# The delta heads' base inverses stay on the chip: turned by VectorE and copied into level tiles

## The chip, the cores and the metric

The kernel runs on one core of a Trainium2 chip. The metric is the device time of one launch in microseconds, the median of several runs. The core's engines are TensorE (PE in the profile, its weight loads PEld), VectorE (DVE), ScalarE (ACT), GpSimd (POOL) and SyncE (SP), which issues the transfers of this kernel; 16 DMA engines carry them.

## The reference

One layer of a bidirectional encoder for 1024 tokens of width 1024, in float32: a mixer of windowed attention and gated DeltaNet side by side, then cross-attention into 256 memory tokens, then a SwiGLU block. The change lies in the DeltaNet part, which solves a unit lower triangular system for each head, direction and chunk of 64 tokens:

```python
kb = k * beta[..., None]
lower = jnp.where(strict, jnp.einsum('bhnid,bhnjd->bhnij', kb, k) * decay, 0.0)
tmat = lower + jnp.eye(c, dtype=jnp.float32)
rhs = jnp.concatenate([v * beta[..., None], kb * jnp.exp(g)[..., None]], axis=-1)
sol = lax.linalg.triangular_solve(tmat, rhs, left_side=True, lower=True, unit_diagonal=True)
```

There are 4 heads and 2 directions. The kernel works on blocks of 128 tokens (8 of them, NT), and inverts the triangle instead of solving.

## The kernel before

**Stages.** The first stage projects the delta heads' keys, queries and values, convolves them, and forms the products of keys (`ORDER_1`, up to about 215 us). The second (`ORDER_2`, up to about 370 us) projects the attention heads' columns (`A`), values (`V`) and the delta heads' gates (`G`), runs the first attention windows (`W`) and the levels of the inverses (`L0` to `L3`, one for each head). The third (`ORDER_3`) runs the recurrent scans over the eight blocks, with the remaining windows and the projections of the memory between their steps. Cross-attention and the SwiGLU block follow. The tokens in `ORDER_1` to `ORDER_3` give the order of the program text. A scheduler lays out each engine's instructions ahead of the launch (`schedule_with_timeline_sim=True`); on the chip each engine and SP's queue runs its own instructions in that order.

**Base inverses.** The heads are taken in two groups g of two. `base_inverse(g)` (tokens `B0`, `B1`) inverts all diagonal blocks of 32x32 of a group at once: 2 directions x 2 heads x 8 blocks of 128 tokens x 4 blocks of 32 give 128 systems, one on each partition, in a tile A of [128, 32, 32]. A forward substitution on VectorE (L581 and L583, 30 steps) runs on A in place. Then the unit diagonal is set (L584), and the columns are multiplied by beta twice: on VectorE into V with rows and columns swapped (L585), and on GpSimd into A itself (L586).

**The way through DRAM.** On each partition a block of 32x32 lies along the free dimension. The levels need it with its rows on partitions. For that A and V are written to DRAM tensors: `d_m5` holds blocks of 32x32, and `d_lv` holds images of whole level tiles in which the blocks lie on the diagonal (`diagonal`, L591 to L595; ten issues for each group, in pieces of 32 elements for `d_lv`). All the rest of an image has to be zero, so eight transfers from a zeroed tile clear `d_lv` early in the first stage (`clear`, L453, tokens `Z` in `ORDER_1`). `levels(h)` reads `d_m5` once (L605) and a tile DZ of [128, 4, 4, 128] for each half of the blocks (L615, 1 MB each). DZ holds four images: D5 and D6, the left factors of the two levels, and Z for each direction, which becomes the result.

**Levels.** A part b of `levels(h)` covers four blocks of 128 tokens. It loads the key products Ul (L618), transposes them on TensorE (L622) and masks them into L5 and L6 on VectorE (L623, L624). `pair` is a product with L on TensorE (L631), an eviction on ScalarE (L633), and a product with D5 or D6 (L637). The first pair joins blocks of 32 to 64: z5 (L642) is put into D6 by two VectorE transposes (L643, L644) and into Z by copies (L645, L646, L650, L651). mov6 (L648, L649) is read from Z for the second pair, which joins 64 to 128 and writes the last quarters of Z (L653, L654). Z is stored to `d_pz` (L656) for the scans. The two parts run interleaved, and products of the projections (L289) stand between their steps on TensorE.

**Neighbours.** The rotary embedding of the attention columns (L785 to L792) makes two products on VectorE, swaps halves by four transfers `rr<-rr` (L790), adds (L791) and stores (L792). The gate's activation (L811, L812) uses the same tile tag as the rotary sum. Each projection loads its weights (L125), and splits them in two parts on ScalarE (L103) and VectorE (L104). A window loads its queries (L671), splits them on ScalarE and GpSimd (L673, L674) and goes on with scores on TensorE and VectorE.

## Time and profile before

| | |
|---|---|
| median of three runs | 1529.46 us (1528.9 to 1532.73) |
| the profiled execution | 1530.58 us, span 1528.9 us |
| mean granted TensorE clock | 0.989 |
| DMA | 276.26 MB, mean 181 GB/s |
| packets under 512 B | 39264 of 287335 |
| the first stage's stretch from 20 to 200 us | TensorE busy 179.2 of 180 us |

The profile gives busy time for each engine, and for stretches of time; the times of single instructions on each queue; in brackets the time an engine stood idle ahead of an instruction, and the event that ended this. A matmul's end is modelled, so a TensorE that counts as busy can still lose time: its starts and its clock tell more. "SPq" rows are issues on SP's queue, and their time is what the issue held the queue for.

### The profile page before, as it was taken

To read this page: it belongs to the slowest core of one execution; us is meant where nothing else is said; L and a number is where in the kernel's file an instruction comes from. 1 tells how busy PE (TensorE), PEld (TensorE's weight loads), DVE (VectorE), ACT (ScalarE), POOL (GpSimd) and SP (SyncE) were. 2 spreads that over 40 slices of the span, in tenths; PEclk is the share of its full clock that TensorE was granted. 3 is DMA by queue.
4 is the path that set the end of the run, shared out by engine and by line. 5 is a ranking of instruction groups with operands and counts; after the bars stand their busy time and mean duration, and the time that the engine had idled before them with its cause. 6 is when DMAs were issued, how large, how long until landed. Compare 5 with 4: busy or idle time off the path is not lost.

```text
span 1528.9 us, 21239 instructions
## 1 busy us (share of the span) xinstructions
PE 1479.8 (97%) x7437; PEld 1244.3 (81%) x7437; DVE 1092.5 (71%) x1795; ACT 756.5 (49%) x1556; POOL 329.9 (22%) x301
## 2 busy tenths in 40 slices
PE   7999999899999999999999999999999999999998
PEld 6888877787999778888788867888888888888787
DVE  5878998466888866538567768676867775696666
ACT  7678821346567755455545685223232332454533
POOL 0011210101237203152201101433434342000020
PEclk9999999899999999999999999999999999999999
DMA  6844596975998675458734654343434333853355
GB/s 192 298 117 128 146 242 187 235 206 177 336 308 260 199 240 184 134 170 274 237 102 162 203 178 132 104 138 111 149 105 160 124 103 105 321 208 98 109 177 167
DMA packets 287335, 276.26 MB, mean 181 GB/s; under 512 B 39264, under 2 KB 211453, under 8 KB 287229
## 3 DMA queue, kind: packets, MB, share of 16 engines
q1 hardware_dynamic: 287229, 274.92, 57.0%
q8 instruction: 58, 0.95, 0.3%
q14 instruction: 48, 0.39, 0.1%
HBM read 187.54 MB, written 84.71 MB: 178 GB/s over the span
## 4 chain that ended last, share of the span: by engine, by line
PE 64%; DVE 7%; DMA 7%; SPq 3%; issue 2%; ACT 2%; POOL 1%; DVEq 0%; ACTq 0%; POOLq 0%
PE pE L1509 7%; PE pD L1509 7%; PE pmg L1099 6%; PE pdX L1715 6%; PE pA L1509 6%; PE pst L1315 5%; PE pcq L289 4%; PE pdA L1715 4%; PE pB L1509 3%; PE psc L838 3%; PE pdD L1715 2%; PE pg L289 2%; PE pco L1214 1%; DMA qr<-d_q 1%; DMA wraw<-in_w_gate_up_dram 1%
## 5 line engine op out<-in xcount | busy, mean ns | idle before, releaser
L103 ACT CAST whi<-wraw 128x1024 fp32r<-128x1024 f32 x96 | 100.8, 1050 | 133.4 <-DMA wraw<-in_w_gate_up_dram 39.8
L289 PE MATMUL pg<-hhi,whi 128*128 128x512 f32 x352 | 142.2, 404 | 0.0
L289 PE MATMUL pg<-hlo,whi 128*128 128x512 f32 x352 | 142.2, 404 | 0.0
L289 PE MATMUL pg<-hhi,wlo 128*128 128x512 f32 x352 | 140.7, 400 | 0.0
L104 POOL TENSOR_TENSOR wlo<-wraw,whi 128x1024 fp32r<-128x1024 f32 x36 | 88.4, 2455 | 190.1 <-ACT whi L103 181.5
L1509 PE MATMUL pA<-b,whi 128*128 128x512 f32 x352 | 110.9, 397 | 3.6 <-ACT m L1536 2.8
L104 DVE TENSOR_TENSOR wlo<-wraw,whi 128x1024 fp32r<-128x1024 f32 x60 | 73.6, 1227 | 45.2 <-ACT whi L103 44.1
L1509 PEld LDWEIGHTS pA<-b,whi 128*128 128x128 f32 x352 | 65.8, 189 | 18.9 <-ACT m L1536 4.1
L289 PEld LDWEIGHTS pg<-hhi,whi 128*128 128x128 f32 x352 | 67.9, 193 | 13.5 <-ACT hhi L254 0.3
L289 PEld LDWEIGHTS pg<-hhi,wlo 128*128 128x128 f32 x352 | 67.8, 193 | 12.9
L289 PEld LDWEIGHTS pg<-hlo,whi 128*128 128x128 f32 x352 | 67.6, 192 | 12.5
L1715 PE MATMUL pdX<-dhl,whi 128*128 128x512 f32 x264 | 76.1, 390 | 1.5 <-DVE zv L1774 0.7
L1509 PE MATMUL pA<-b,wlo 128*128 128x512 f32 x176 | 69.4, 395 | 0.5 <-DVE wlo L104 0.5
L103 ACT CAST whi<-araw 128x1024 fp32r<-128x1024 f32 (+1 forms) x36 | 35.3, 981 | 67.7 <-PE pdX L1715 27.6
L1592 POOL TENSOR_TENSOR act<-act,up 128x512 f32<-128x512 f32 x33 | 50.7, 1537 | 82.1 <-DVE up L1591 60.8
L104 DVE TENSOR_TENSOR wlo<-araw,whi 128x1024 fp32r<-128x1024 f32 (+1 forms) x36 | 40.8, 1133 | 36.7 <-ACT whi L103 36.5
L314 DVE SCALAR_TENSOR_TENSOR acc<-cp,cols,acc 128x1024 f32<-128x1024 f32 x48 | 63.7, 1330 | 1.5 <-ACT acc L312 1.2
L1564 POOL TENSOR_TENSOR sr<-wraw 128x512 f32<-128x512 f32 x22 | 29.9, 1360 | 151.8 <-DMA wraw<-in_w_gate_up_dram 100.3
L1715 PEld LDWEIGHTS pdX<-dhl,whi 128*128 128x128 f32 x264 | 49.3, 188 | 12.7 <-issue 1.1
L103 ACT CAST dhl<-b 128x512 fp32r<-128x512 f32 x66 | 40.3, 620 | 31.7 <-PE pdA L1715 13.5
L1509 PE MATMUL pB<-s0h,s1h 128*128 128x512 f32 x176 | 54.4, 390 | 0.3 <-ACT s1h L103 0.3
L1509 PE MATMUL pE<-b,s2h 128*128 128x512 f32 x176 | 54.2, 389 | 0.0
(495 smaller groups left out, 4199.7 us busy)
## 6 DMA issues: line engine op xcount, KB each, us to landing
wraw<-in_w_gate_up_dram SPq DMA_DIRECT2D x54, 512.0 KB, 3.8
kv<-d_kv SPq DMA_DIRECT2D x32, 512.0 KB, 8.0
wraw<-in_w_in_dram SPq DMA_DIRECT2D x22, 512.0 KB, 6.5
b<-in_w_down_dram SPq DMA_DIRECT2D x20, 512.0 KB, 6.0
araw<-d_as SPq DMA_DIRECT2D x20, 512.0 KB, 3.6
d_lv<-zero SPq DMA_DIRECT2D x8, 1024.0 KB, 8.9
DZ<-d_lv SPq DMA_DIRECT2D x8, 1024.0 KB, 8.9
pz<-d_pz SPq DMA_DIRECT2D x32, 256.0 KB, 6.5
```

Of the source, the lines that this page charges most:

```text
L103: nc.scalar.copy(hi, src)
L104: return (eng or nc.vector).tensor_tensor(lo, src, f32(hi), ALU.subtract)
L289: nc.tensor.matmul(p_, w[:, k, :], ah[a][:, k, :], start=(k == 0 and i == 0), stop=(k == nk - 1 and i == 2))
L314: nc.vector.scalar_tensor_tensor(acc, cp[:, t:t + S], taps[t], acc, ALU.mult, ALU.add)
L838: nc.tensor.matmul(out[:, d, h, :], lt[:, d, h, :], rt[:, d, h, :], start=True, stop=True)
L1099: nc.tensor.matmul(pp[t], act[a][:, k, tt], w_[:, kk, :], start=(k == 0 and i == 0), stop=(k == KT - 1 and i == 2))
L1214: nc.tensor.matmul(po, vr_[a][:, kt, cs], pts[kt][b_], start=(kt == 0 and i == 0), stop=(kt == 1 and i == 2))
L1315: nc.tensor.matmul(bank, a[:, tt], w, start=(start and i == 0), stop=(stop and i == 2), skip_group_check=not check)
L1509: nc.tensor.matmul(out_, w[a][:, k, :], xx[b_][:, k, :], start=(start and k == 0 and i == 0), stop=(k == HK - 1 and i == 2), skip_group_ch ...
L1564: nc.gpsimd.tensor_tensor(s[0], b_[:, 0:HK], b_[:, HK:], ALU.add)
L1592: nc.gpsimd.tensor_tensor(o_, o_, up, ALU.mult)
L1715: nc.tensor.matmul(banks[t], a[:, k - k0, tt], w, start=(first and k == 0 and i == 0), stop=(k == NB - 1 and i == 2), skip_group_check=not ...
```

## The change

In `base_inverse` the multiplication by beta is done once, on VectorE and in place in A, and the unit diagonal is set there too. `turn_base` makes two tiles of it, `turned_base[0]` and `[1]`, with one VectorE transpose of 32x32 blocks each, one of them reading A with rows and columns swapped. For group 0 it is called at the end of `base_inverse(0)`, for group 1 at the head of `levels(2)`. `block_of` gives the view of these tiles that holds one block for several chunks; its elements are 32 apart.

The DRAM tensors `d_lv` and `d_m5` go, with the clears, the scatter and the loads. m5 is filled by four ScalarE copies for each level. The images D, Z0 and Z1 of each half are tiles that exist once for the whole stage and are cleared once on GpSimd. D serves both levels: four ScalarE copies set its diagonal blocks for the first pair, and between the pairs two GpSimd copies replace its second and third block. From the second head on, the two corners that the level before has filled are cleared again. Eight GpSimd copies set the diagonals of Z0 and Z1.

The rest is room: a pool `wt` holds A and the two turned tiles, shared with `abT` and with the work tiles of the rotary angles, the positions are loaded in one transfer, V has one buffer for both groups, and z5 and mov6 have two buffers each.

```diff
@@ -34,7 +34,7 @@
 
 
 
-ORDER_1 = ("k0 k1 Z E0 Z K0 Z U0 Z E1 Z K1 Z U1 Z S0 q0 Z v0 q1 C0 v1 E2 C1 k2 E3 k3 q2 K2 U2 v2 K3 U3 S1 q3 C2 v3 C3 B0 B1").split()
+ORDER_1 = ("k0 k1 E0 K0 U0 E1 K1 U1 S0 q0 v0 q1 C0 v1 E2 C1 k2 E3 k3 q2 K2 U2 v2 K3 U3 S1 q3 C2 v3 C3 B0 B1").split()
 ORDER_2 = "L0 L1 A4 V A0 A1 G0 G1 L2 L3 W W W A2 A3 G2 G3 W".split()
 ORDER_3 = ("M " + "s01 W K " * 5 + "s01 K " * 3 + "s01 V V").split()
 
@@ -148,6 +148,7 @@
     p1 = ExitStack()
     hx = p1.enter_context(pool("hx", 1, side="right"))
     trp = p1.enter_context(pool("trp", 2, side="right"))
+    wt = p1.enter_context(pool("wt", 1, side="right"))
     pcv = ExitStack()
     tcv = pcv.enter_context(pool("tcv", 2, side="right"))
     pa0 = ExitStack()
@@ -185,20 +186,6 @@
     d_pz = [[dram.tile([NT, P, 2, 2, P], F32, name=f"d_pz{g}{d}") for d in range(2)] for g in range(2)]
     d_u = [dram.tile([2, NT, P, P], F32, name=f"d_u{g}") for g in range(2)]
 
-    LW, LB_ = 4 * P, 32 * 4 * P + 32
-    d_lv = [dram.tile([1, 8 * NT * LB_ + LW], F32, name=f"d_lv{g}") for g in range(2)]
-    d_m5 = [dram.tile([8 * NT, 32, 32], F32, name=f"d_m5{g}") for g in range(2)]
-
-    def diagonal(g, kind):
-
-        at = kind * P
-        return (d_lv[g][0, at:at + 8 * NT * LB_].rearrange("(n y) -> n y", y=LB_)[:, 0:32 * LW]
-                .rearrange("n (r w) -> n r w", w=LW)[:, :, 0:32])
-
-    def level_rows(g, x0):
-
-        return (d_lv[g][0, 0:8 * NT * LB_].rearrange("(x y) -> x y", y=4 * LB_)[x0:x0 + 4, 0:P * LW]
-                .rearrange("x (p w) -> p x w", w=LW))
     d_beta = [dram.tile([32, P], F32, name=f"d_beta{g}") for g in range(2)]
     d_mix = dram.tile([D, S], F32, name="d_mix")
     d_mk = dram.tile([D, ML], F32, name="d_mk")
@@ -339,7 +326,7 @@
         nc.vector.tensor_scalar(wabr, hT[0][0].bitcast(F32)[:, :, 0:P], 0.0, None, ALU.mult)
     nc.vector.tensor_copy(wabr[:, :, 0:16], wab)
     nc.vector.tensor_tensor(wabr[:, :, 16:32], wab, f32(wabr[:, :, 0:16]), ALU.subtract)
-    abT = tb.tile([32, S], F32, tag="A", name="abT", bufs=1)
+    abT = wt.tile([32, S], F32, tag="A", name="abT")
     for hf in range(2):
         pp = pg.tile([P, 512], F32, tag="pg", name="pg")
         for k in range(KT):
@@ -409,14 +396,14 @@
     c3 = float(np.float32(2 * math.pi - c1 - c2))
     sct = ra.tile([P, 2, S], F32, tag="sct", name="sct")
     sinT, cosT = sct[:, 0], sct[:, 1]
+    posi = wt.tile([P, S], I32, tag="inv1", name="posi")
+    nc.sync.dma_start(posi, positions[0].partition_broadcast(P))
     for hf in range(2):
         sl = slice(hf * HALF, (hf + 1) * HALF)
-        posi = t1.tile([P, HALF], I32, tag="posi", name="posi", bufs=1)
-        nc.sync.dma_start(posi, positions[0, sl].partition_broadcast(P))
-        ang = t1.tile([P, HALF], F32, tag="ang", name="ang", bufs=1)
-        nc.vector.tensor_copy(ang, posi)
+        work = wt.tile([P, 2, HALF], F32, tag="inv0", name="ang")
+        ang, rn = work[:, 0], work[:, 1]
+        nc.vector.tensor_copy(ang, posi[:, sl])
         nc.vector.tensor_scalar(ang, ang, rope_f, None, ALU.mult)
-        rn = t1.tile([P, HALF], F32, tag="rn", name="rn", bufs=1)
         nc.vector.tensor_scalar(rn, ang, 1.0 / (2.0 * math.pi), MAGIC, ALU.mult, ALU.add)
         nc.vector.tensor_scalar(rn, rn, MAGIC, None, ALU.subtract)
         for cc in (c1, c2, c3):
@@ -430,7 +417,6 @@
 
     pa1.close()
     pa0.close()
-    tb1 = pp_.enter_context(pool("tb1", 1))
 
 
 
@@ -442,15 +428,6 @@
     nEG = sm.tile([P, 2, 4, NT], F32, name="nEG")
     nc.vector.tensor_scalar(nEG, EG[:, 0], -1.0, None, ALU.mult)
 
-    zero = t2.tile([P, 4, P], F32, tag="vt", name="zero").rearrange("p c n -> p (c n)")
-    nc.gpsimd.memset(zero, 0.0)
-    cleared = [0]
-
-    def clear():
-
-        g, x0 = cleared[0] // 4, 4 * (cleared[0] % 4)
-        cleared[0] += 1
-        nc.sync.dma_start(level_rows(g, x0), bc(zero, 1, (P, 4, LW)))
 
 
     def together(gens):
@@ -558,7 +535,7 @@
 
 
 
-        V = (tb1 if g else tb).tile([P, 32, 32], F32, tag="V", name="V", bufs=1)
+        V = tb.tile([P, 32, 32], F32, tag="V", name="V", bufs=1)
         for q in range(4):
             r = slice(32 * q, 32 * q + 32)
             nc.sync.dma_start(V[q:64:4], d_u[g].rearrange("h c p n -> (h c) p n")[:, r, r])
@@ -568,7 +545,7 @@
         for d in range(2):
             nc.sync.dma_start(bB[64 * d:64 * d + 64], bv[d])
         nc.sync.dma_start(b1, bv[1])
-        A = tb.tile([P, 32, 32], F32, tag="A", name="A", bufs=1)
+        A = wt.tile([P, 32, 32], F32, tag="A", name="A")
         nc.vector.scalar_tensor_tensor(A[0:64], V[0:64].rearrange("p r s -> p s r"), -1.0,
                                        bc(bB[0:64], 1, (64, 32, 32)), ALU.mult, ALU.mult)
         nc.vector.scalar_tensor_tensor(A[64:128], V[0:64], -1.0, bc(b1, 1, (64, 32, 32)), ALU.mult, ALU.mult)
@@ -581,18 +558,25 @@
             nc.vector.tensor_tensor(tv, A[:, j + 1:, j:j + 1].to_broadcast([P, n, j]),
                                     A[:, j:j + 1, 0:j].to_broadcast([P, n, j]), ALU.mult)
             nc.vector.tensor_tensor(A[:, j + 1:, 0:j], A[:, j + 1:, 0:j], tv, ALU.add)
-        nc.gpsimd.memset(A.rearrange("p r s -> p (r s)")[:, 0:1024:33], 1.0)
-        nc.vector.tensor_tensor(V.rearrange("p r s -> p s r"), A, bc(bB, 2, (P, 32, 32)), ALU.mult)
-        nc.gpsimd.tensor_tensor(A, A, bc(bB, 2, (P, 32, 32)), ALU.mult)
-
-        for d in range(2):
-            first, second = (A, V) if d == 0 else (V, A)
-            lo_, hi_ = 64 * d, 64 * d + 64
-            nc.sync.dma_start(d_m5[g][1 - d::2], second[lo_ + 1 - d:hi_:2])
-            nc.sync.dma_start(diagonal(g, 0)[d::2], first[lo_ + d:hi_:2])
-            nc.sync.dma_start(diagonal(g, 2 + d), second[lo_:hi_])
-            for q in (2 * d, 2 * d + 1):
-                nc.sync.dma_start(diagonal(g, 1)[q::4], first[lo_ + q:hi_:4])
+        nc.vector.memset(A.rearrange("p r s -> p (r s)")[:, 0:1024:33], 1.0)
+        nc.vector.tensor_tensor(A, A, bc(bB, 2, (P, 32, 32)), ALU.mult)
+        bases.append(A)
+        if g == 0:
+            turn_base()
+
+    bases, turned_base = [], []
+
+    def turn_base():
+
+        turned_base[:] = [wt.tile([P, 32, 32], F32, tag=f"inv{i}", name=f"inv{i}") for i in range(2)]
+        A = bases.pop()
+        nc.vector.transpose(turned_base[1], A)
+        nc.vector.transpose(turned_base[0], A.rearrange("p r s -> p s r"))
+
+    def block_of(kind, d, hh, b, cs):
+
+        q = 64 * d + 32 * hh
+        return turned_base[kind][q:q + 32].rearrange("p x (c b) -> p b c x", b=4)[:, b, cs]
 
     def levels(h):
 
@@ -601,8 +585,11 @@
         def blocks(name):
             return tl_.tile([P, NT, 32], F32, tag=name, name=name, bufs=1)
 
+        if bases and h == 2:
+            turn_base()
         m5 = blocks("m5")
-        nc.sync.dma_start(m5, d_m5[g][32 * hh:32 * hh + 32].rearrange("(c b) r s -> (b r) c s", b=4))
+        for q in range(4):
+            nc.scalar.copy(m5[32 * q:32 * q + 32], block_of(q % 2, 1 - q % 2, hh, q, slice(0, NT)))
 
         def part(b):
             c4 = slice(4 * b, 4 * b + 4)
@@ -611,9 +598,21 @@
                 return tl_.tile([P, 4, P], F32, tag=name, name=name, bufs=2)
 
             L5, L6 = wide("L5"), wide("L6")
-            DZ = tl_.tile([P, 4, 4, P], F32, tag="DZ", name="DZ", bufs=3)
-            nc.sync.dma_start(DZ.rearrange("p c k n -> p c (k n)"), level_rows(g, hh * NT + 4 * b))
-            D5, D6, Z = DZ[:, :, 0], DZ[:, :, 1], [DZ[:, :, 2 + d] for d in range(2)]
+            D5, *Z = images[b]
+            D6 = D5
+
+            def put(copy, dst, q, kind, d):
+                x = slice(32 * q, 32 * q + 32)
+                copy(dst[x, :, x], block_of(kind, d, hh, q, c4))
+
+            if h:
+                nc.gpsimd.memset(D5[32:64, :, 0:32], 0.0)
+                nc.gpsimd.memset(D5[64:96, :, 96:128], 0.0)
+            for q in range(4):
+                put(nc.scalar.copy, D5, q, q % 2, q % 2)
+            for d in range(2):
+                for q in range(4):
+                    put(nc.gpsimd.tensor_copy, Z[d], q, 1 - d, d)
             Ul = wide("Ul")
             nc.sync.dma_start(Ul, d_u[g][hh, c4].rearrange("c p n -> p c n"))
             yield
@@ -638,13 +637,15 @@
                 return p_
 
             p_ = yield from pair(L5, m5[:, c4, :], D5, 32)
-            z5 = tl_.tile([P, 4, 32], F32, tag="z5", name="z5", bufs=1)
+            z5 = tl_.tile([P, 4, 32], F32, tag="z5", name="z5", bufs=2)
             nc.scalar.mul(z5, p_, -1.0)
+            put(nc.gpsimd.tensor_copy, D6, 1, 0, 0)
+            put(nc.gpsimd.tensor_copy, D6, 2, 1, 1)
             nc.vector.transpose(D6[32:64, :, 0:32], z5[0:32])
             nc.vector.transpose(D6[64:96, :, 96:128], z5[96:128])
             nc.vector.tensor_copy(Z[1][32:64, :, 0:32], z5[32:64])
             nc.vector.tensor_copy(Z[0][64:96, :, 96:128], z5[64:96])
-            mov6 = tl_.tile([P, 4, 64], F32, tag="mov6", name="mov6", bufs=1)
+            mov6 = tl_.tile([P, 4, 64], F32, tag="mov6", name="mov6", bufs=2)
             nc.scalar.copy(mov6[0:64], Z[1][0:64, :, 0:64])
             nc.vector.tensor_copy(mov6[64:128], Z[0][64:128, :, 64:128])
             nc.scalar.copy(Z[0][0:32, :, 32:64], z5[0:32])
@@ -758,9 +759,8 @@
         for o in order:
             table[o[0]](*(int(c) for c in o[1:]))
 
-    issue(ORDER_1, {**{n: delta_proj(n) for n in "kqv"}, "Z": clear, "E": decays, "K": turned_keys, "U": key_products, "S": beta_rows,
+    issue(ORDER_1, {**{n: delta_proj(n) for n in "kqv"}, "E": decays, "K": turned_keys, "U": key_products, "S": beta_rows,
                     "C": query_products, "B": base_inverse})
-    assert cleared[0] == 8
     pp_.close()
     pcv.close()
     pss.close()
@@ -770,6 +770,9 @@
     tw.tile([P, 384], F32, tag="sc", name="sc", bufs=8)
     vhl = tw.tile([P, NT + 1, 2, 2, 64], F32R, tag="vhl", name="vhl", bufs=1)[:, 0:NT]
     tl_ = p1.enter_context(pool("tl", 2))
+    images = [[tl_.tile([P, 4, P], F32, tag=f"{n}{b}", name=n, bufs=1) for n in ("D", "Z0", "Z1")] for b in range(2)]
+    for t in images[0] + images[1]:
+        nc.gpsimd.memset(t, 0.0)
 
     def pair():
         t = ra.tile([P, 2, HALF], F32, tag="rr", name="rr", bufs=2)
```

## The prediction

> **What bounds the kernel now.** I read the busy table and the slices first, then the stretches of 20 us around the edit, then each TensorE stop there with the queue behind it.
>
> ```profile
> PE 1479.8 (97%) x7437; PEld 1244.3 (81%) x7437; DVE 1092.5 (71%) x1795; ACT 756.5 (49%) x1556; POOL 329.9 (22%) x301
> ```
>
> TensorE is the bound, and the edit leaves its matmuls as they are in number and shape. So it can only give or take TensorE's stops and the low clock behind them. The stretches (columns: length, busy of PE, PEld, DVE, ACT, POOL with counts, granted clock, DMA share, GB/s):
>
> ```profile
> 40.00:60.00 20.00, 20.00 (x93) 16.10 (x92) 19.55 (x30) 10.51 (x16) 0.27 (x4) 1.00 1.03 373
> 60.00:80.00 20.00, 20.00 (x96) 16.75 (x95) 14.36 (x28) 14.73 (x29) 0.13 (x2) 1.00 0.57 181
> 200.00:220.00 20.00, 20.00 (x95) 16.28 (x94) 19.55 (x28) 5.79 (x21) 3.89 (x4) 1.00 0.87 192
> 220.00:240.00 20.00, 17.03 (x87) 14.35 (x87) 15.26 (x35) 2.24 (x7) 0.00 (x0) 0.91 1.05 312
> 240.00:260.00 20.00, 19.45 (x108) 16.22 (x106) 17.89 (x45) 4.54 (x11) 0.15 (x1) 1.00 0.37 104
> 260.00:280.00 20.00, 18.61 (x101) 15.34 (x99) 12.33 (x19) 4.74 (x9) 1.92 (x1) 1.00 0.95 226
> 280.00:300.00 20.00, 15.91 (x78) 13.46 (x78) 6.24 (x18) 9.35 (x24) 2.74 (x3) 0.82 0.94 263
> 300.00:320.00 20.00, 20.00 (x107) 17.39 (x107) 11.92 (x29) 7.68 (x23) 2.79 (x3) 0.93 0.82 235
> ```
>
> From 200 to 320 us, where the levels run, TensorE stands idle 2.97 + 0.55 + 1.39 + 4.09 = 9.0 us. The clock of 0.91, 0.82 and 0.93 costs at most 0.09, 0.18 and 0.07 of 20 us each, 6.8 us; part of that falls on idle time, so I count 6. DMA is near its full share in the same stretches. The four long stops, in brackets with their releasers, and what stood in front of them on SP, ACT, DVE and POOL:
>
> ```profile
> 223.05 0.66 PE L622 MATMUL ps<-ident,Ul 128*128 128x128 f32 x4 [2.97 <-DMA Ul<-d_u]
> 265.73 0.66 PE L622 MATMUL ps<-ident,Ul 128*128 128x128 f32 x4 [1.39 <-DVE DZ L654]
> 281.20 1.10 PE L631 MATMUL ps<-mov,L 128*128 128x64 f32 x8 [1.15 <-ACT mov L648]
> 297.18 1.12 PE L622 MATMUL ps<-ident,Ul 128*128 128x128 f32 x4 [2.48 <-DVE DZ L654]
> ```
>
> ```profile
> 197.60 0.49 SPq L591 DMA_DIRECT2D d_m<-V  x1
> 205.80 1.34 SPq L595 DMA_DIRECT2D d_lv<-V  x1
> 217.22 0.45 SPq L618 DMA_DIRECT2D Ul<-d_u  x1
> 264.52 4.27 SPq L592 DMA_DIRECT2D d_lv<-V  x1
> 272.44 2.81 SPq L595 DMA_DIRECT2D d_lv<-V  x2
> 276.52 0.53 SPq L792 DMA_DIRECT2D d_q<-rop  x1
> 281.38 0.58 SPq L615 DMA_DIRECT2D DZ<-d_lv  x1
> ```
>
> ```profile
> 279.64 0.60 ACT L811 ACTIVATE gt<-pg 128x512 f32<-128x512 f32 x1 [5.52 <-DMA d_q<-rop]
> 295.77 0.62 ACT L673 CAST qs<-qr 128x512 fp32r<-128x512 f32 x1 [2.23 <-DMA qr<-d_q]
> ```
>
> ```profile
> 262.75 1.92 POOL L586 TENSOR_TENSOR A<-A,bB 128x1024 f32<-128x1024 f32 x1 [3.40 <-DMA d_pz<-DZ]
> 254.92 0.69 DVE L791 TENSOR_TENSOR rop<-rop,rr 128x512 f32<-128x512 f32 x1 [0.27 <-DMA rr<-rr]
> 263.17 2.04 DVE L791 TENSOR_TENSOR rop<-rop,rr 128x512 f32<-128x512 f32 x1 [0.51 <-DMA rr<-rr]
> ```
>
> The reader is to see that all four lead back to work which the edit removes. **Stop one**: Ul is issued only at 217, after SP has spent 197.6 to 207.1 on the scatter of base 0, and lands beside the first DZ loads. **Stop two**: the rope add takes 2.04 us where it else takes 0.69, since it stands until POOL's multiply L586 ends at 262.75 + 1.92 = 264.67; L654 and the release of the PSUM bank follow it. **Stop three**: the gate's activation waits for the store d_q, held on SP to 276.5 behind the scatter of base 1, and mov of the level is behind it on ACT. **Stop four**: ACT waits for a window's qr load with DMA full (0.94), a DZ load of 1 MB among it, and the level's last step is behind that wait.
>
> **The change part by part.**
>
> *Clears.* Eight issues of 1 MB each go from the front.
>
> ```profile
> d_lv<-zero SPq DMA_DIRECT2D x8, 1024.0 KB, 8.9
> DZ<-d_lv SPq DMA_DIRECT2D x8, 1024.0 KB, 8.9
> ```
>
> At 40 to 60 us they fill DMA (1.03), but TensorE is busy for all 20.00 us, so I take 0. PEld is 16.10 against 16.75 in the next stretch, 0.65 us that could be hidden loss: bounds 0 and -0.8. Positions in one load and the shared tiles change no count of DVE work there: 0.
>
> *Scatter and DZ loads.* Twenty scatter issues, four m5 and eight DZ loads go. Their worth is the stops: -9.0 - 6 = **-15 us** if nothing takes their place. The bound below it is the 0.8 of the clears on top.
>
> *DVE.* A base loses the multiply L585 and gains the contiguous multiply, a small memset and two transposes.
>
> ```profile
> L585 DVE TENSOR_TENSOR V<-A,bB x2: 2070/2082/2093, 195.5 to 260.6; 128x1024 f32<-128x1024 f32 x2
> L104 DVE TENSOR_TENSOR wlo<-wraw,whi x8: 1194/1221/1626, 197.4 to 318.0; 128x1024 fp32r<-128x1024 f32 x8
> L643 DVE STREAM_TRANSPOSE DZ<-z x8: 301/301/302, 242.5 to 351.9; 32x128 f32<-32x128 f32 x8
> L645 DVE COPY DZ<-z x8: 216/217/219, 243.5 to 352.6; 32x128 f32<-32x128 f32 x8
> ```
>
> The contiguous multiply is like wlo, 1.22. No transpose of 1024 columns is shown: at the least it is one pass like wlo, 1.22; at the most eight of the small ones, 8 x 0.301 = 2.41. The one that reads with a stride I put by L585, 2.08, the other at 1.3, since the small one is 0.08 above the copy of its size. With 0.1 for the memset that is 1.22 + 0.1 + 1.3 + 2.08 - 2.08 = **+2.6 us** a base, bounds +1.7 and +4.1. DVE is busy 19.55 of 20 around base 0, so rope work behind it comes 2.6 later; TensorE did not wait for it there (20.00), so 0 to +2.6, and I take 0. In exchange POOL's 2.32 us multiply leaves the chain, and with it stop two.
>
> *ACT.* Sixteen copies of 32x256 for m5 and 32 of 32x128 for D.
>
> ```profile
> L648 ACT COPY mov<-DZ x8: 390/406/407, 243.8 to 357.5; 64x256 f32<-64x256 f32 x8
> L650 ACT COPY DZ<-z x8: 280/298/300, 238.8 to 351.9; 32x128 f32<-32x128 f32 x8
> ```
>
> 16 x 0.41 + 32 x 0.30 = 16 us. Their read has a stride that these rows lack; twice that, 32 us, is the other bound (DVE's L585 is 1.7 times its contiguous kin). ACT is busy 2.2 to 9.4 of 20 us here, which covers either sum. Without the cover each level pays 4 us ahead of its first pair. The copies into D wait for the last matmul that reads it in the level before, as its only image now; behind a wait of that kind stand weight casts and evictions on ACT.
>
> *POOL.* Sixty-four copies into Z, sixteen into D between the two pairs, 12 memsets of corners, six whole ones.
>
> ```profile
> L674 POOL TENSOR_TENSOR qs<-qr,qs 64x512 fp32r<-64x512 f32 x8 | 10.4, 1297 | 81.3 <-ACT qs L673 80.9 <-DVE nm L689 0.4
> 298.19 0.20 POOL L694 TENSOR_TENSOR es<-prm,m 128x4 f32<-128x4 f32 x1 [0.47 <-DVE m L684]
> L446 POOL MEMSET zero<- 128x512 f32 x1 | 0.5, 524 | 0.0
> 259.19 0.15 POOL L584 MEMSET A<- 128x32 f32 x1 [44.06 <-DVE A L583]
> ```
>
> A tiny operation is 0.20, and 128 columns of L674's 512 are 0.32: bounds 0.20 and 0.52, and I take 0.4 for one copy. 80 x 0.4 + 12 x 0.15 + 6 x 0.52 = 37 us over some 150, on an engine that stood idle for 44 us there. Eight copies, 3.2 us, stand ahead of a part's mov, beside its transpose and first pair. If they are late, TensorE stops at L631, since its order is fixed. The copies into Z also wait for the store d_pz of the level before; nothing but windows' qs (1.30 each) stands behind them. Base 1's transposes wait on DVE until L1's copies have read the turned tiles, with rope adds and the masks L623 behind them, which TensorE needs for its next bank.
>
> Here is the weak spot: POOL and DVE. Stop two showed a DVE add waiting for POOL's whole instruction. So 80 copies can hold up DVE, and be held up by it. In place of the four stops I put two new ones, one for each pair of levels, of the mean size of the old, 15 / 4 = 3.75 us: **+7.5 us**. Bounds: none, and the rival below.
>
> The Trainium skill has a rule on this, in "SBUF — State Buffer", section "Who interferes with whom": a VectorE instruction with two SBUF inputs and a GpSimd instruction that reads SBUF exclude each other for the whole instruction, and the second to start stands still. The trace agrees (2.04 us for 0.69). It speaks against copies on POOL beside the long DVE loop of base 1; by it the sum would be that of the lock's rival below, 1536 us, and by the rows' mean stop 1522.
>
> *The sum* is made against the profiled execution: 1530.6 us, with a span of 1528.9, against a median of 1529.5; the differences of 1.1 and less do not matter. -15 + 7.5 = -7.5, so 1529.5 - 7.5 = **1522 us**.
>
> **The rivals.** *Full gain.* The levels run from engines alone, POOL keeps up, no new stop: 1529.5 - 15 = 1514.5 us. For it:
>
> ```profile
> L637 PE MATMUL ps<-bs,DZ x128: 190/275/323, 237.4 to 366.3; 128*128 128x32 f32 x64, 128*128 128x64 f32 x64
> L583 DVE TENSOR_TENSOR A<-A,tmpb x60: 191/346/410, 136.5 to 260.3; 128x30 f32<-128x30 f32 x4, 128x58 f32<-128x58 f32 x4, 128x84 f32<-128x84 f32 x4, 128x108 f32<-128x108 f32 x4
> ```
>
> Base 0 is ready for its multiplies at 195.5 (L585's first start), but its first product with D runs at 237.4, 42 us later, most of it spent on the way through DRAM. DMA loses 8 MB of loads there, and by the code 2 x 8,192 pieces of 128 bytes. Against: the order on TensorE is fixed ahead, so any late copy is a stop.
>
> *Stops handed on.* The transfers were hidden in effect: with them gone, TensorE stops at the next late thing (Ul, qr and the rope's rr loads are still there, DVE is at 19.55) and the 15 us come back: 1529.5 us, 1525 to 1534. That SP and DMA stand in three of the four stops speaks against it.
>
> *The lock, on the other side.* DVE's loop of base 1, up to 260.3, is one of small two-input adds, and each POOL copy waits for one and holds up the next. With a wait of 0.4 (an add of L583 takes 0.35 to 0.41) a part's eight copies take 6.4 us in place of 3.2. That decides where mov comes later than its slot on TensorE. At 3.2 us a part, half covered, eight parts give 13 us idle, and the low clock (6 us for 9 before) adds 8: 13 + 8 - 15 = +6, so 1536 us; with no cover 26 + 17 - 15 = +28. For it: stop two. Against: base 1's loop ends before L2, so half of the parts see less of it.
>
> **How the numbers follow.** Full gain 0.20, forecast 0.33 (1517 to 1525), handed on 0.15, lock 0.32. What a measurement here can tell from no change is 0.3%, 4.6 us, so the line of faster is 1524.9 and of slower 1534.1. Faster: 0.20 + 0.32 of the forecast; same: 0.15 and the forecast's last 0.01; slower 0.32. The range takes in full gain with a bit of the clears and a copy or two less late, 1511, and the lock to less than half of its uncovered price, 1542; less than 0.2 is outside. The likeliest case's own range is 1517 to 1525.
>
> **What would show it.** Right: no stop before L622 on Ul at the first level; SP without 1 to 4 us issues at 197 to 207 and 264 to 275; DMA share of 200 to 320 near 0.5; clock 1.00 but for one or two dips. Copies of 0.4 on POOL, transposes of 1.3 and 2.1 on DVE. The lock: DVE adds of L583 well over 0.4 beside POOL copies, copies over 0.6, and stops at L631 released by mov. The prediction is wrong if TensorE's idle time from 200 to 320 does not fall below 9 us, or if the time is lost after 380 us, where the scans run.

## The result and the profile after

The changed kernel takes 1537.74 us (median of four runs, 1535.31 to 1540.26) where the kernel before takes 1529.18 us (four runs). The ratio is 1.0053, with a 95% interval of 1.0028 to 1.0078: slower by 0.53%, 8 us, where the forecast was 1522. The profiled execution is one of 1540.26 us with a span of 1538.0 us and a mean granted clock of 0.989, the same clock as before.

The page of the kernel after, busy time of each engine:

```profile
PE 1481.9 (96%) x7437; PEld 1245.3 (81%) x7437; DVE 1095.6 (71%) x1801; ACT 787.4 (51%) x1608; POOL 364.7 (24%) x394
```

TensorE has the same 7437 matmuls. VectorE's total rose by 3 us, ScalarE's by 31 and GpSimd's by 35. GpSimd's is near the 37 us of the prediction; ScalarE's is at the prediction's upper bound of 32, twice the 16 taken. The engines' sums don't tell where the 8 us go; TensorE's stops do. The stretches of the kernel after (columns: length, busy of PE, PEld, DVE, ACT, POOL with counts, granted clock, DMA share, GB/s):

```profile
20.00:40.00 20.00, 16.16 (x74) 12.87 (x74) 15.17 (x32) 12.91 (x24) 0.00 (x0) 0.84 0.31 85
...
220.00:240.00 20.00, 18.77 (x106) 15.82 (x105) 17.02 (x37) 10.44 (x22) 9.06 (x21) 1.00 0.57 165
240.00:260.00 20.00, 20.00 (x110) 17.02 (x109) 18.26 (x49) 10.31 (x21) 3.53 (x9) 1.00 0.52 138
260.00:280.00 20.00, 19.15 (x108) 16.31 (x107) 13.49 (x23) 6.95 (x17) 10.64 (x18) 1.00 0.56 165
280.00:300.00 20.00, 18.51 (x82) 15.39 (x81) 6.50 (x12) 8.54 (x18) 7.76 (x21) 0.83 0.54 163
300.00:320.00 20.00, 19.20 (x117) 16.78 (x116) 11.67 (x36) 11.62 (x29) 4.66 (x8) 1.00 0.26 74
```

and the one stretch of the kernel before that the prediction did not look at:

```profile
20.00:40.00 20.00, 20.00 (x107) 16.77 (x106) 12.15 (x26) 14.69 (x29) 0.00 (x0) 1.00 0.38 103
```

Two things stand there. The levels' stretch did what was forecast: idle from 220 to 320 us is 1.23 + 0 + 0.85 + 1.49 + 0.80 = 4.4 us where it was 9.0, and the DMA share is 0.26 to 0.57 where four of the five stretches had 0.82 to 1.05. One dip of the clock, to 0.83, stays. But from 20 to 40 us, where nothing of the inverses runs, TensorE lost 3.84 us of time and a clock of 0.84, and before it had lost nothing. What happened is on the queues of SP, VectorE and TensorE of the kernel after:

```profile
19.75 0.43 SPq L400 DMA_DIRECT2D posi<-in_positions_dram  x1
...
27.19 0.43 DVE L405 CAST ang<-posi 128x512 f32<-128x512 int32 x1 [4.66 <-DMA posi<-in_positions_dram]
27.65 0.49 DVE L406 TENSOR_SCALAR ang<-ang,CE 128x512 f32<-128x512 f32 x1
28.05 0.75 DVE L233 TENSOR_SCALAR xt<-xt,rs 128x1024 f32<-128x1024 f32 x1
...
31.18 2.14 DVE L410 SCALAR_TENSOR_TENSOR ang<-ang 128x512 f32<-128x512 f32 x3
...
28.86 0.77 PE L239 MATMUL ps<-ident,xt 128*128 128x128 f32 x5 [0.94 <-DVE xt L233]
...
34.49 1.11 PE L239 MATMUL ps<-ident,xt 128*128 128x128 f32 x4 [2.79 <-DVE hlo L242]
```

and of the kernel before:

```profile
36.22 0.34 SPq L415 DMA_DIRECT2D posi<-in_positions_dram  x1
...
39.75 0.43 DVE L417 CAST ang<-posi 128x512 f32<-128x512 int32 x1 [3.10 <-DMA posi<-in_positions_dram]
```

The rotary angles are now worked out 12 us earlier. VectorE stands 4.66 us in front of the positions' load, with the scaling of x (L233) behind it in its queue, and puts more angle work in front of the low parts hlo (L242). TensorE, which needs both for the first projections, stops behind each of them. By the code, what moved them is the memory of their tiles: the positions and angles lay in a pool whose memory the tiles of x held until they were done, and now lie in the pool `wt`, free from the start. (The positions also come in one load in place of two; e2 below keeps two.)

To follow the loss through the kernel I added up, for stretches of 20 us, TensorE's idle time and the time that the clock cost (20 minus busy, plus 20 times one minus the clock). The sums from the start, in us, each from one profiled execution; the columns e1 to h2 are kernels of the experiments:

| up to | before | after | e2 | e1 | f4 | f9 | g9 | h1 | h2 |
|---|---|---|---|---|---|---|---|---|---|
| 60 us | 9.0 | 15.4 | 12.3 | 8.8 | 8.9 | 8.8 | 8.8 | 8.9 | 8.3 |
| 200 us | 9.7 | 17.0 | 12.3 | 10.7 | 11.2 | 10.5 | 9.4 | 11.1 | 12.5 |
| 320 us | 25.5 | 24.7 | 28.4 | 18.5 | 18.1 | 18.0 | 26.6 | 18.0 | 17.5 |
| 420 us | 33.8 | 34.8 | 34.7 | 31.2 | 26.8 | 32.0 | 38.2 | 26.1 | 24.3 |
| 600 us | 44.6 | 50.7 | 47.3 | 40.8 | 40.7 | 44.8 | 61.4 | 39.0 | 37.5 |
| 980 us | 56.1 | 63.5 | 62.8 | 52.2 | 52.3 | 56.5 | 72.7 | 50.8 | 47.8 |

After against before: +6.4 by 60 us, +7.3 by 200, then -8.1 over the levels (7.7 lost between 200 and 320 us, where before loses 15.8), and +8 between 320 and 980. A single execution can differ from its kernel's median: h2's took 1520.41 us where its median is 1525.9.

### The profile page after: what moved, and what is told of

Read it like the earlier page. It is cut to its first block, busy times and chain, and to the rows that moved or that the text cites. A ratio compares the mean times of both kernels' runs of the same rounds, so it can differ in the third digit from the quotient of the medians.

```text
span 1538.0 us, 21325 instructions
## 1 busy us (share of the span) xinstructions
PE 1481.9 (96%) x7437; PEld 1245.3 (81%) x7437; DVE 1095.6 (71%) x1801; ACT 787.4 (51%) x1608; POOL 364.7 (24%) x394
## 4 chain that ended last, share of the span: by engine, by line
PE 70%; DVE 10%; DMA 8%; ACT 6%; issue 4%; SPq 2%; POOL 0%; DVEq 0%; ACTq 0%; POOLq 0%
PE pg L276 9%; PE pE L1512 8%; PE pD L1512 8%; PE pA L1512 6%; PE pmg L1102 6%; PE pdX L1718 5%; PE pst L1318 5%; PE pB L1512 4%; PE pcq L276 3%; PE pdA L1718 2%; PE psc L841 2%; PE pdD L1718 2%; DMA wpart<-in_w_co_dram 1%; DMA b<-in_w_down_dram 1%; PE pco L1217 1%
## 5 line engine op out<-in xcount | busy, mean ns | idle before, releaser
L1595 POOL TENSOR_TENSOR act<-act,up 128x512 f32<-128x512 f32 x33 | 50.8, 1538 | 83.2 <-DVE up L1594 61.8
L104 DVE TENSOR_TENSOR wlo<-araw,whi 128x1024 fp32r<-128x1024 f32 (+1 forms) x36 | 40.8, 1133 | 36.8 <-ACT whi L103 36.7
L103 ACT CAST s0h<-sr 128x512 fp32r<-128x512 f32 x22 | 13.7, 622 | 80.7 <-POOL sr L1567 80.2
```

The lines of the kernel that those rows point to most:

```text
L103: nc.scalar.copy(hi, src)
L104: return (eng or nc.vector).tensor_tensor(lo, src, f32(hi), ALU.subtract)
L1595: nc.gpsimd.tensor_tensor(o_, o_, up, ALU.mult)
```

## The experiments

Times are medians; each ratio is against the kernel before, run on the same chip beside it.

**e1: the angles late again.** In the changed kernel the first angle instruction is put behind the last hlo on VectorE's queue:

```diff
-        nc.vector.tensor_copy(ang, posi[:, sl])
+        with tc.issue_after(cut.ins):
+            nc.vector.tensor_copy(ang, posi[:, sl])
```

> The changed kernel with one order added: VectorE starts the first rotary angle only behind the last normalised part of the second half of the tokens, as it did in the kernel before. Theory A (the shared tiles set the angle work free, it runs ahead of the normalisation at 22 to 41 us and TensorE starts 5 to 7 us late): TensorE busy in 20 to 40 us goes from 16.2 back to 19.5 or more, and the time falls by 5 to 8 us, to 1530 to 1533. Rival B (the lock between GpSimd's copies and VectorE): the start gets better but the time stays at 1536 to 1539. Rival C (order on ScalarE late in the second stage sets the end of that stage whatever went before): the start gets better by 6 us and the time by less than 3.

1531.27 us, ratio 1.0004 (0.9988 to 1.0019). The kernel is level with before, 0.5% under the changed one. The edit orders one instruction, but the scheduler then laid out the rest anew: of TensorE's 7437 matmuls 562 stand at another place than in the changed kernel (the fewest that would have to be moved to make the two orders alike), most of them after 300 us. So the whole 0.5% can't be put down to the angles by e1 alone. Its first stretch has no loss left:

```profile
20.00:40.00 20.00, 20.00 (x107) 16.72 (x106) 15.75 (x33) 15.33 (x29) 0.00 (x0) 1.00 0.31 88
```

**e2: that part alone in the kernel before.** The tiles of positions and angles go to a pool that is free from the start; the rest of the text is the kernel before. TensorE's order changes little, in 62 of 7437 matmuls. On SP's queue the clears of `d_lv` come earlier too, from 28.30 us in place of 36.66:

```diff
-        posi = t1.tile([P, HALF], I32, tag="posi", name="posi", bufs=1)
+        posi = early.tile([P, HALF], I32, tag="posi", name="posi")
...
-        ang = t1.tile([P, HALF], F32, tag="ang", name="ang", bufs=1)
+        ang = early.tile([P, HALF], F32, tag="ang", name="ang")
...
-        rn = t1.tile([P, HALF], F32, tag="rn", name="rn", bufs=1)
+        rn = early.tile([P, HALF], F32, tag="rn", name="rn")
```

> The kernel before with one part of the change alone: positions, angles and their work tile lie in a pool that waits for no other tile, so that their work may run early; everything else as before, transfers through DRAM too. Theory A: TensorE busy in 20 to 40 us falls from 20.0 to about 16, and the time rises by 5 to 8 us, to 1534 to 1538. Rivals B and C: no change beyond 2 us.

1538.4 us, ratio 1.0039 (1.0023 to 1.0054): 6 us by the interval's middle, without anything of the inverses. The stretch in its profile, and the same wait and the same stop on VectorE and TensorE:

```profile
20.00:40.00 20.00, 16.51 (x86) 12.59 (x85) 15.11 (x34) 14.99 (x29) 0.00 (x0) 1.00 0.82 278
```

```profile
26.93 0.43 DVE L417 CAST ang<-posi 128x512 f32<-128x512 int32 x1 [4.53 <-DMA posi<-in_positions_dram]
...
34.71 0.66 PE L252 MATMUL ps<-ident,xt 128*128 128x128 f32 x4 [1.83 <-DVE hlo L255]
```

The first positions have landed at 26.93, before the first clear is issued, and TensorE's stops in this stretch are ended by xt, hhi and hlo, so the earlier clears are not their cause. Taken out of the changed kernel the early angles give back 7.5 us (1.0053 to 1.0004), put into the kernel before they cost 6 (3.5 to 8 by the interval). So early angles alone make a slowdown of the size seen. Where it is lost is only half followed: in e2's profile 3.3 us by 60 us, and 3.8 more after 320. Of the 8 us that the table shows lost between 320 and 980 us in the kernel after, e1 loses only 3 (52.2 - 18.5 = 33.7 against 30.6 before). Why a late start costs more there was not tried.

**e3: GpSimd's copies on VectorE.** The three calls that set blocks of the images, in the changed kernel:

```diff
-                    put(nc.gpsimd.tensor_copy, Z[d], q, 1 - d, d)
+                    put(nc.vector.tensor_copy, Z[d], q, 1 - d, d)
...
-            put(nc.gpsimd.tensor_copy, D6, 1, 0, 0)
-            put(nc.gpsimd.tensor_copy, D6, 2, 1, 1)
+            put(nc.vector.tensor_copy, D6, 1, 0, 0)
+            put(nc.vector.tensor_copy, D6, 2, 1, 1)
```

> The changed kernel with its 80 small copies on VectorE instead of GpSimd. Rival B (the lock): VectorE's adds of base 1 go back from 20.9 to 19.9 us in sum and the time falls by 4 us or more, to 1534 or less. Theory A: the time moves by less than 4 us, in either direction, since VectorE gets 80 x 0.22 = 18 us more work in exchange for an end to waits of 1 us in its loop.

1546.93 us, ratio 1.0094 (1.0069 to 1.012): 6 us slower than the changed kernel by the ratios, whose intervals just overlap. That is more than either theory allowed; VectorE is busy 14 us more from 200 to 320 us (101.0 for 87.0). So taking the copies off GpSimd in this way is no cure. The 120 adds of the two bases, which the lock should have lengthened, by lines in the kernels before, after and e3 (sum and mean ns after the bar):

```profile
L581 DVE TENSOR_TENSOR tmpb<-A 128x30 f32<-128x30 f32 (+14 forms) x60 | 19.8, 330 | 1.4
L583 DVE TENSOR_TENSOR A<-A,tmpb 128x30 f32<-128x30 f32 (+14 forms) x60 | 19.8, 329 | 1.3
```

```profile
L558 DVE TENSOR_TENSOR tmpb<-A 128x30 f32<-128x30 f32 (+14 forms) x60 | 20.3, 339 | 2.5 <-POOL A L552 1.2
L560 DVE TENSOR_TENSOR A<-A,tmpb 128x30 f32<-128x30 f32 (+14 forms) x60 | 20.3, 338 | 1.2
```

```profile
L560 DVE TENSOR_TENSOR A<-A,tmpb 128x30 f32<-128x30 f32 (+14 forms) x60 | 19.8, 330 | 1.2
L558 DVE TENSOR_TENSOR tmpb<-A 128x30 f32<-128x30 f32 (+14 forms) x60 | 19.7, 329 | 2.4 <-POOL A L552 1.2
```

They cost 40.6 us with the copies on GpSimd, 39.6 before and 39.5 with the copies on VectorE. That fits the lock, and on these adds it is worth 1 us; in e1, with the same copies in another order, they take 41.5.

**f4, f6, f7: the copies into Z done more than once.** On top of e1, all 64 twice (f4), those of the first two heads twice (f6), all three times (f7):

```diff
-                    put(nc.gpsimd.tensor_copy, Z[d], q, 1 - d, d)
+                    for _ in range(2):
+                        put(nc.gpsimd.tensor_copy, Z[d], q, 1 - d, d)
```

> e1_angles_late with each of the 64 copies of a turned block into an image done twice on GpSimd (the second writes the same values): 64 more copies of 0.4 to 0.5 us, about 30 us more of GpSimd. Rival B of the prediction (GpSimd's copies keep VectorE off the shared port, and that is what the change costs): VectorE's instructions beside them get longer, and the time rises by as much as that rival gave for the whole set, 10 us or more. Theory A (the copies lie beside other work): VectorE's base adds sum to at most 1 us more each, and the time rises by 0 to 3 us.

> e1_angles_late with the copies of turned blocks into the images done twice for the first two heads alone: 32 more copies of 0.46 us, half of those of f4_copies_twice, which came out at 1526.4 us, 4 us under e1_angles_late. Theory E (more GpSimd work moves the order that the planner gives every engine; the time is that of an order, and has no slope with the number of copies): anywhere from 1526 to 1535 us, not midway by rule. Rival F (the copies themselves help, by holding back stores or VectorE where that is of use): midway, 1528 to 1529.5 us.

> e1_angles_late with each of the 64 copies done three times: 128 more copies of 0.46 us, 59 us more of GpSimd. Theory E (order): anywhere from 1526 to 1535 us. Rival F (the copies help): 1522 to 1525 us. Rival B (the copies cost by the shared port, and f4_copies_twice was lucky): 1532 us or more, with VectorE's base adds longer than in e1_angles_late.

| | copies added | us | ratio |
|---|---|---|---|
| f6 | 32 | 1527.33 | 0.9983 (0.9966 to 1.0001) |
| f4 | 64 | 1526.36 | 0.9976 (0.9963 to 0.999) |
| f7 | 128 | 1554.03 | 1.0151 (1.0125 to 1.0178) |

Copies in vain make e1 faster, then much slower. For f6, theory E (the scheduler's order sets the time) and rival F (the copies themselves help) lie too near each other: its interval holds the middle between e1 and f4. In f4 the group is twice as long and each copy no longer than in e1 (e1, then f4):

```profile
L607 POOL COPY Z<-inv 32x128 f32<-32x128 f32 x64 | 29.2, 457 | 14.1 <-DMA d_pz<-Z 11.0
```

```profile
L607 POOL COPY Z<-inv 32x128 f32<-32x128 f32 x128 | 58.3, 456 | 24.0 <-DMA d_pz<-Z 17.3
```

So 29 us more on GpSimd lie beside other work: f4 is faster, where rival B (the lock) had it 10 us or more slower, and its adds take 42.5 us for e1's 41.5. f7 speaks against rival F and is as slow as rival B asked, with longer adds too (43.1 us). But 1.6 us of adds are not the 23 us that it lies over e1, and its trace shows the loss elsewhere: from 320 to 420 us TensorE is idle for 20.1 us at a clock of 0.83, where e1 has 9.1 us and 0.97. There the copies no longer fit: GpSimd runs 28 of them in a row ahead of the last level's blocks of D, and TensorE stands behind the level (POOL, then PE):

```profile
351.30 12.61 POOL L607 COPY Z<-inv 32x128 f32<-32x128 f32 x28
...
368.71 1.97 PE L632 MATMUL ps<-mov,L 128*128 128x64 f32 x8 [4.28 <-ACT mov L651]
...
409.61 0.80 PE L983 MATMUL pck<-mT,whi 128*128 128x256 f32 x2 [6.21 <-ACT whi L103]
```

The first stop is the one that the prediction named for late copies (TensorE waits for mov), at three times their number. The second waits for a weight that was loaded late; whether the copies made it late was not followed.

**f1 and f5: ScalarE's turns between Exp and Silu.** In the changed kernel's profile ScalarE loads a function table nine times from 195 to 390 us, before five times, and e1 five times too, where the expectation supposed some nine. f1 is e1 with the gates' function replaced, f5 is e1 with all gates ahead of the windows:

```diff
-            nc.scalar.activation(gt, pp[hf], AF.Silu)
+            nc.scalar.activation(gt, pp[hf], AF.Identity)
```

```diff
-ORDER_2 = "L0 L1 A4 V A0 A1 G0 G1 L2 L3 W W W A2 A3 G2 G3 W".split()
+ORDER_2 = "L0 L1 A4 V A0 A1 G0 G1 L2 L3 G2 G3 W W W A2 A3 W".split()
```

> e1_angles_late with the gates' Silu replaced by the identity: it leaves out the gate's nonlinearity on d_gate. Question: with the angles late, the levels' stretch of the profiled execution is ahead of before by 6.7 us of TensorE idle and lost clock at 320 us and by 2.6 us at 420 us; what takes the rest. Theory C (ScalarE's turn between the windows' Exp and the gates' Silu, 1.28 us for each of some 9 table loads between 195 and 390 us, sets the end of stage 2): at least 4 loads go, TensorE's idle between 340 and 420 us falls from 8.4 us to 5 us or less, and the time lies 3 to 5 us under e1_angles_late (1526 to 1528 us). Theory D (VectorE and the loads of stage 3 set the stretch, whatever ScalarE does): loads go, the idle stays within 1.5 us of 8.4 us, and the time is within 2 us of e1_angles_late.

> e1_angles_late with the last two gate projections ahead of the windows in stage 2, so that ScalarE goes from Silu to Exp once (nothing left out). Theory C: table loads between 195 and 390 us fall from 9 or so to 5 or fewer, and the time is 2 to 4 us under e1_angles_late, under both kernels. Theory D: no gain from the loads, and the last windows have two projections fewer to lie under, so the same to 4 us over.

f1: 1530.64 us, ratio 1.0016 (1.0001 to 1.0032). f5: 1537.94 us, ratio 1.0055 (1.0033 to 1.0077). From 340 to 420 us, e1 and then f1:

```profile
340.00:420.00 80.00, 71.62 (x480) 64.83 (x481) 59.17 (x155) 47.52 (x107) 19.97 (x25) 0.96 0.79 237
```

```profile
340.00:420.00 80.00, 69.38 (x460) 62.48 (x461) 56.16 (x147) 42.20 (x99) 19.03 (x23) 0.96 0.79 233
```

With one load left ScalarE works 5 us less, and TensorE's idle time is 10.6 us where it was 8.4, in the same order of all matmuls as in e1. Theory C falls: ScalarE's time for the loads is not what TensorE waits for. Theory D had the time right and the idle time not (it rose by 2.2 us, not by less than 1.5). f5 has one load left as well, and is 7 us slower than e1, beyond the 4 us of theory D. D's reason, that the windows have two projections fewer to lie under, was not shown.

**f3, f9, g9: the order at the start of stage 3.** f3 and f9 are e1, g9 is the kernel before:

```diff
-ORDER_3 = ("M " + "s01 W K " * 5 + "s01 K " * 3 + "s01 V V").split()
+ORDER_3 = ("s01 M W K " + "s01 W K " * 4 + "s01 K " * 3 + "s01 V V").split()   # f3
+ORDER_3 = ("M W " + "s01 W K " * 4 + "s01 K " * 4 + "s01 V V").split()         # f9, g9
```

> e1_angles_late with stage 3 begun by a scan step and two windows ahead of the memory's normalization and its 16 turned tiles (which in e1_angles_late take the first four of five PSUM banks and VectorE ahead of the scans). Theory D (the normalization holds VectorE and the banks when the scans could start): the stop of 2.67 us at 372 us behind mT goes, the first scan products start with the first kv (about 375 us), and the time is 2 to 4 us under e1_angles_late. Theory C or a start set by the loads of kv and pz (8.4 us each with the DMA engines full): the scans wait as long as before with less work to cover it, and the time is the same or up to 5 us over.

> e1_angles_late with one pair of windows ahead of the first scan step (stage 3 begins M W s01 W K, the last of the five pairs moves up, nothing added): window products under which the first loads of kv and pz can lie. If the lead of the levels' stretch is lost because the first scan steps wait for loads with too little beside them, TensorE's idle between 360 and 420 us falls from 7.5 us to 4 us or less and the time lies 2 to 4 us under both e1_angles_late and before (1526 to 1528 us). If VectorE sets that stretch, the windows ahead only delay the scans: the same to 4 us over.

> The kernel before with the same order of stage 3 as f9_windows_at_scan_start and nothing else. It is what that order is worth without the change: if f9 gains and this doesn't, the gain is the levels' lead kept; if both gain alike, it is the order's own, and the change's levels are worth nothing here. Theory: level with before to 3 us over (its scans start 6 to 8 us later and wait less).

f3: 1547.07 us, ratio 1.0117 (1.0095 to 1.014). f9: 1531.65 us, ratio 1.0009 (0.9992 to 1.0025). g9: 1545.59 us, ratio 1.0107 (1.0078 to 1.0137). In f3 the stop behind mT goes and the scans start at 374 us, behind a wait of 2.91 us for kv, as theory D had it. But the time is some 17 us over e1, which neither theory allowed; so D falls, and the size was not explained. f9 has no gain either: its idle from 360 to 420 us is 9.2 us where e1 has 7.5. What g9 shows was not expected: an order that costs the kernel before 16 us costs the kernel with the new levels next to nothing. Most of its loss comes at the end of the scans, where weights are late for TensorE:

```profile
556.61 1.20 PE L994 MATMUL pcv<-whi,mT 128*128 128x512 f32 x4 [2.48 <-ACT whi L103]
567.90 0.80 PE L1099 MATMUL pmg<-whi,s0h 128*128 128x512 f32 x1 [5.21 <-ACT whi L103]
```

So what the levels seem worth depends on the order around them: nothing that can be measured by e1 against before, 14 us by f9 against g9. The two edits are not alike in effect, though: the same new order of stage 3 moved 255 matmuls in g9 and 35 in f9, so the 14 us can be the scheduler's as much as the levels'.

**h1, h2, i1: the copies' engine.** On top of e1: D's first copies on GpSimd (h1), those of m5 too (h2), or D's copies twice on ScalarE (i1):

```diff
-                put(nc.scalar.copy, D5, q, q % 2, q % 2)
+                put(nc.gpsimd.tensor_copy, D5, q, q % 2, q % 2)                  # h1, h2
...
-            nc.scalar.copy(m5[32 * q:32 * q + 32], block_of(q % 2, 1 - q % 2, hh, q, slice(0, NT)))
+            nc.gpsimd.tensor_copy(m5[32 * q:32 * q + 32], block_of(q % 2, 1 - q % 2, hh, q, slice(0, NT)))   # h2
```

```diff
-                put(nc.scalar.copy, D5, q, q % 2, q % 2)
+                for _ in range(2):
+                    put(nc.scalar.copy, D5, q, q % 2, q % 2)                     # i1
```

> e1_angles_late with the 16 copies of a turned block into a D image on GpSimd in place of ScalarE: some 7 us of ScalarE (16 of 0.42 us) go, GpSimd takes 16 more of 0.43 us, a quarter of what f4_copies_twice put on it in vain. If ScalarE's copies are what the levels' stretch and the start of stage 3 still wait for, TensorE's idle between 200 and 420 us falls from 14.1 us by 2 us or more and the time lies 2 to 5 us under before. If only the planner's order moves the time (theory E), anywhere from 1526 to 1535 us, with ScalarE's lighter load without a trace in the idle.

> h1_d_copies_on_gpsimd with the 16 copies of four blocks each into m5 (0.65 us each on ScalarE) on GpSimd too: together 17 us less of ScalarE and some 20 us more of GpSimd, two thirds of what f4_copies_twice added without harm, but these stand ahead of the first level's products. If the copies' place is right: as h1 or up to 3 us better. If GpSimd is late with them: TensorE waits behind m for each head, some 2 us four times, and the time is 1533 to 1540 us.

> e1_angles_late with each of the 32 copies of a turned block into a D image done twice on ScalarE (the second writes the same values): 13.5 us more of ScalarE, where h1_d_copies_on_gpsimd took 13.5 us off and gained 4 us. If ScalarE's load in the levels' stretch is what eats their lead, TensorE's idle between 200 and 420 us rises from 15.1 us by 3 us or more and the time lies 3 to 8 us over before (1532 to 1537 us). If only the planner's order moves the time, as the copies done twice on GpSimd suggest (f6 and f4: 10.5 us of idle, 2.5 to 4 us under before), the idle may fall as well as rise, and the time is anywhere from 1525 to 1533 us.

| | us | ratio |
|---|---|---|
| h1 | 1525.18 | 0.9973 (0.9955 to 0.999) |
| h2 | 1525.9 | 0.9969 (0.9953 to 0.9986) |
| i1 | 1526.66 | 0.9982 (0.997 to 0.9994) |

(D's copies are 32, 13.5 us of ScalarE; the expectation of h1 counted half of them, and put e1's idle time at 14.1 us where it is 15.1.) h1 and h2 beat both kernels, by 0.3% the kernel before and by 0.8% the changed one. By themselves they look like the case for ScalarE's load. The stretches of e1, h1, h2 and i1:

```profile
200.00:320.00 120.00, 113.95 (x603) 96.04 (x600) 93.31 (x193) 57.63 (x138) 40.66 (x83) 0.99 0.49 142
320.00:420.00 100.00, 90.92 (x594) 81.48 (x595) 72.16 (x183) 60.22 (x136) 28.38 (x44) 0.97 0.79 233
```

```profile
200.00:320.00 120.00, 116.45 (x618) 99.07 (x617) 97.04 (x200) 46.61 (x107) 51.86 (x108) 0.97 0.50 144
320.00:420.00 100.00, 91.91 (x636) 82.89 (x635) 73.58 (x183) 57.45 (x133) 31.49 (x51) 1.00 0.85 250
```

```profile
200.00:320.00 120.00, 116.79 (x635) 99.16 (x633) 99.24 (x198) 38.66 (x101) 68.14 (x129) 0.99 0.53 148
320.00:420.00 100.00, 95.03 (x648) 86.71 (x647) 78.61 (x197) 61.88 (x137) 32.56 (x46) 0.98 0.84 250
```

```profile
200.00:320.00 120.00, 114.70 (x585) 96.84 (x585) 91.63 (x190) 66.55 (x161) 41.62 (x83) 0.93 0.50 140
320.00:420.00 100.00, 94.11 (x623) 85.02 (x623) 72.08 (x184) 65.98 (x144) 30.57 (x44) 0.98 0.76 235
```

From e1 to h1 and h2 ScalarE's busy time from 200 to 320 us falls from 57.6 to 46.6 and 38.7 us, and TensorE's idle time from 200 to 420 us with it, from 15.1 to 11.6 and 8.2. But i1 puts the same 13.5 us on ScalarE, has 11.2 us of idle time, and gains 3 us too. So the load is not what decides. What f4, f6, h1, h2 and i1 have in common is only that a copy more or elsewhere changes the order that the scheduler gives the engines: of TensorE's 7437 matmuls, 183 (i1) to 454 (h2) stand at another place than in e1. Six orders of nearly the same work, e1's among them, lie between 1525 and 1531 us; that the order is the cause is what is left, and was not shown by an edit that changes the order alone at that place.

## Why the prediction was wrong

**The step that failed** is the last sentence on the clears: "Positions in one load and the shared tiles change no count of DVE work there: 0". The count did not change, the time did. A tile's memory is also a wait, and in the kernel before this wait held the positions and the angle work back until x was done. In the pool `wt` they were free to run ahead, and stood in front of x's scaling and hlo. Cost: 3.84 us idle and a clock of 0.84 from 20 to 40 us in the profile, 6 us alone (e2), up to 7.5 us in the change (e1, whose order differs elsewhere too). That is close to half of the 15.7 us between 1522 and 1537.74; most of the other half is the levels' gain of 7.5 us, which did not reach the end. The row that would have told it is in the trace of before: the positions issued at 36.22, after x's work, which had to have a reason. I looked for none, since TensorE was at 20.00 of 20 there.

**The levels' term was right in size, to 320 us.** -15 for the four stops and +7.5 for new ones made -7.5; the profile of after has -8.1 between 200 and 320 us and e1 -8.0. The 7.7 us left in the profile of after are 4.4 us of idle time and 3.4 us of clock; two stops of the old mean size would be 4.5 and 3. That it fits so well is in part luck: in i1's profile, with 5.3 us of idle time, more dips of the clock bring the loss there to 13.9 us. Three of the four stops of before are gone, the one behind mov is 0.85 where it was 1.15, and the DMA share is 0.5, as forecast. The stops that the levels now have are small, four of 3.6 us of idle time together (the one behind mov among them), where two new ones were put:

```profile
231.29 1.05 PE L630 MATMUL ps<-m,L 128*128 128x32 f32 x8 [0.77 <-DVE L L623]
232.79 1.05 PE L630 MATMUL ps<-m,L 128*128 128x32 f32 x8 [0.45 <-DVE L L623]
275.15 1.08 PE L630 MATMUL ps<-mov,L 128*128 128x64 f32 x8 [0.85 <-DVE mov L650]
281.90 2.82 PE L636 MATMUL ps<-bs,D 128*128 128x64 f32 x16 [1.49 <-ACT bs L632]
```

**It did not reach the end whole.** The prediction named this as what would make it wrong ("if the time is lost after 380 us"), and priced it only in the rival of stops handed on: 1529.5 us, which is where e1 lies. In e1, of the lead of 7 us at 320 us, 2.6 are left at 420; the median is level with before. In f4, f6, h1, h2 and i1 2.5 to 4 us are left by the medians. So the levels alone are worth 0 to 4 us here, about half of the forecast or less. What takes the rest was not found: ScalarE's table loads (f1), its copies (i1) and two orders at the start of stage 3 (f3, f9) were tried, and none gave it back.

**The rivals.** The lock's 1536 us came nearest to 1537.74, by luck: the adds cost 1 us more (against before and e3), doubled copies cost nothing (f4), and of the stops at L630 behind mov that it foretold there is one, of 0.85 us. The rule of the Trainium skill behind it ("SBUF — State Buffer", section "Who interferes with whom") is seen here in small: the adds took 40.6 us for 39.6, and a copy into Z 499 ns in the mean, with a median of 411 and a longest of 1907. So most copies were not held up: 0.09 us for each in the mean, where the rival had put 0.4. Full gain fell with the 4.4 us of idle time that stayed.

**Sizes of single terms.** By operation and tile in the kernel after:

```profile
L573 DVE STREAM_TRANSPOSE inv<-A x2: 1200/1223/1246, 186.9 to 277.0; 128x1024 f32<-128x1024 f32 x2
L574 DVE STREAM_TRANSPOSE inv<-A x2: 1999/2013/2027, 188.1 to 275.0; 128x1024 f32<-128x1024 f32 x2
...
L606 POOL COPY Z<-inv 32x128 f32<-32x128 f32 x64 | 32.0, 499 | 17.1 <-DMA d_pz<-Z 14.1
L606 ACT COPY D<-inv 32x128 f32<-32x128 f32 x32 | 13.4, 420 | 0.5
L592 ACT COPY m<-inv 32x256 f32<-32x256 f32 x16 | 10.7, 668 | 3.5 <-DVE inv L574 2.3 <-PE ps L457 1.0
```

The transposes at 1.22 and 2.01 us were forecast at 1.3 and 2.08. GpSimd's copy at 0.50 stands near the upper bound of 0.52 in the mean; its median of 0.41 is the 0.4 taken. ScalarE's copies are 24 us, not 16: the stride in their read does cost, between the value taken and its bound of 32. The time does not show it: i1 added 13.5 us of such copies to e1 and was not slower.

## What to carry to other kernels

Where a change moves a tile to other memory, look up in the trace what its first writer waited for before: that wait may have kept work in its place, and without it a wait for a load can land at the head of a queue that feeds the bound engine. If the place matters, write it down as an order (`issue_after`), not as a side effect of who shares memory with whom. And where a scheduler lays out the queues, one small edit can reorder hundreds of instructions: judge a part by several variants of it (here 0 to -4 us for nearly the same levels), not by one, and compare the orders of two kernels before a difference is put down to the edit.
